# Where the weight tiles of the q/k units lie: other offsets for the second half unit in a hybrid decoder block

## The chip, the cores and the metric

The kernel runs on one core of a Trainium2 chip. The metric is the device time of one execution in microseconds (us); the time before is the median of three runs. The profile is of one further execution, and its own time stands in the table below.

## The reference, cut to what matters

One layer of a decoder block on x of 256 tokens by 2048 channels, float32: a combined input projection feeds gated linear attention (GLA, 4 heads, key width 256) and forgetting attention (FoX, 8 heads of 128); the two branches are gated, merged and projected, then a layer norm, a gated MLP with a short convolution (width 5632), a second layer norm, and a gated per-layer embedding.

```python
proj = x @ w_in                                   # (256, 2048) @ (2048, 13336)
gq, gk, gv, gr, glr, fq, fk, fv, ff, ma, mb = jnp.split(proj, offsets, axis=-1)
...
log_a = jax.nn.log_sigmoid(glr @ w_gla_lr + b_gla_lr) / GLA_TAU
o  = gla_chunked(gq / 16, gk, gv, log_a)          # GLA branch: q, k of 1024 columns each
of = fox_attention(fq, fk, fv, log_f)             # FoX branch: q, k of 1024 columns each
merged = sigmoid(ma) * (gla(o, gr) @ w_branch_gla) + sigmoid(mb) * (of @ w_branch_fox)
x = layer_norm(ALPHA * x + merged @ w_out)
x = layer_norm(ALPHA * x + (gelu(conv(x @ w_gate)) * (x @ w_up)) @ w_down)
x = x + sigmoid(x @ w_ple_gate) * (p @ w_ple_proj)
```

The change touches how the columns fq, fk, gq and gk of the projection are computed.

## The kernel before

**Precision.** Each float32 product is made of three products of shorter operands. An array v is split into hi, a copy rounded to the type float32r, and lo = v - hi; the product is hi x hi plus hi x lo plus lo x hi. The activations are kept split: tile xT holds for each of the 16 blocks of 128 channels 512 columns, the 256 tokens' hi and beside it their lo. x1T is the same for the MLP's input.

**Units.** All large weights come as units of 128 x 2048 float32 (1 MB), in the order of use, numbered u: 0 to 15 the FoX q and k columns (one q unit and one k unit per head), 16 to 31 the GLA q and k columns (two q, two k per head), 32 to 51 merge gates, then GLA values and output gates, the other merge gates, branch projections, the output projection, from 136 on gate and up columns of the MLP in turn (the first three before the main loop over them), from 224 on the down projection and the embedding's gate. `prep` loads a unit in two halves of 1024 columns. For each half SP issues a DMA into a "raw" slot, ScalarE (ACT) copies it to a hi tile (the helper of line 130), and VectorE (DVE) subtracts to make the lo tile (line 255). `unit` hands out a unit and first prepares up to three ahead. The hi and the lo tiles have pools of their own with six slots each; a slot is 1088 float32 wide (4352 bytes, 17 times 256) for a tile of 1024, and `place(u)` says how many elements into its slot the tile begins. That is all that `place` does.

**The offsets before.** `place` gives (16, 4) elements, that is 64 bytes for hi and 16 bytes for lo, to the q/k units (0 to 31) and to the gate and up units from 139 on; (0, 60), 0 and 240 bytes, to every fourteenth of these, called TURN; (0, 16) to units 136 to 138; and (0, 0) to the rest.

**The matmuls of a q/k or gate/up unit.** `w_unit` uses the weights as stationary operand (what a weight load brings into the array) and the activations as moving operand. For each of 16 blocks there is a pair: `high`, with a hi slice of 128 x 128, streams all 512 columns of the activations (line 320); `low`, with the lo slice, streams the 256 hi columns (line 325). Blocks 0 to 7 read the first half's tiles, blocks 8 to 15 the second half's. A slice is 512 bytes wide. A TURN unit does six pairs, then the remaining low matmuls, then the remaining high ones. Merge gates, branch projections and the down projection work the other way round: activations stationary, weights moving (line 1007 for the merge gates).

**What is slipped in.** In the q/k units a `tick` after the eighth pair of a unit (block 7) runs one step of a generator on the same engines: first the GLA gates (line 582), then the FoX heads (logits line 622, transposes line 649, values lines 656 and 658), then the levels of GLA's attention matrix (line 763). Some steps have matmuls, others don't. The order on TensorE is that of the program; SP's queue of transfers is in program order too. `comb` adds the two halves of a unit's result when it is complete.

Of the kernel before, what the change touches and what calls it, by code (L numbers as in the profile page):

```python
# [36 lines left out]


TURN = range(139, 224, 14)


def place(u):
    if 32 <= u < 136 or u >= 224:
        return 0, 0
    if 136 <= u < 139:
        return 0, 16
    return (0, 60) if u in TURN else (16, 4)


P_STAT = 5000  # L50
# [37 lines left out]
def tile_block(ctx: ExitStack, tc: tile.TileContext, wu, wfv, wpp, xT_in, x_in, pT_in, wlr,  # L88
# [28 lines left out]
    def t1(name):  # L117
        return sm.tile([P, 256], F32, tag="t1", bufs=6, name=name)
# [41 lines left out]
    hS = {}  # L160

    def lo_tile(u, name):
        o = place(u)[1]
        return rlo.tile([P, 1088], F32R, tag="lo", name=f"lo{name}")[:, o:o + 1024]

    def hi_tile(u, name):
        o = place(u)[0]
        return rhi.tile([P, 1088], F32R, tag="hi", name=f"hi{name}")[:, o:o + 1024]

    def differences(r0, r1, h, pinned=False):  # L170
# [28 lines left out]
    def prep_s(u):  # L199
# [25 lines left out]
        def split(src, name, e=slice(0, 1024)):  # L225
            hi = hi_tile(u, f"{u}_{name}")[:, e]
            lo = lo_tile(u, f"{u}_{name}")[:, e]
            copy(hi, src)
            nc.vector.tensor_tensor(lo, src, hi.bitcast(F32), ALU.subtract)  # L229
            return [(hi[:, o:o + 512], lo[:, o:o + 512]) for o in range(0, src.shape[1], 512)]  # L230
# [11 lines left out]
    def prep(pinned=False):  # L242
        u = n_prep[0]
        n_prep[0] += 1
        if u in s_units:
            prep_s(u)
            return
        his, los = [], []
        for h in range(2):
            raw = ring.tile([P, 1024], F32, tag="raw", bufs=5, name=f"raw{u}_{h}")  # L250
            nc.sync.dma_start(raw, wu[u, :, h * 1024:(h + 1) * 1024])
            hi = hi_tile(u, f"{u}_{h}")
            copy(hi, raw)
            lo = lo_tile(u, f"{u}_{h}")
            i = nc.vector.tensor_tensor(lo, raw, hi.bitcast(F32), ALU.subtract)  # L255
            if pinned:
                tc.keep_in_program_order(i)
            his.append(hi)
            los.append(lo)
        ready[u] = (his, los)  # L260
# [53 lines left out]
    def w_unit(ps, hi, lo, act, kts, first, last, tick=None):  # L314
# [13 lines left out]

        turn = n_used[0] - 1 in TURN
        pairs = 6 if turn else n  # L330
# [155 lines left out]
    for u in range(8):  # L486
        hi, lo = fvu[u]
        for j in range(2):
# [8 lines left out]
            for t, i, c in seq:  # L497
                o, n = fch[c]
# [181 lines left out]
    for n in range(16):  # L680
        h, j = n // 2, n % 2
# [115 lines left out]
    for n in range(16):  # L797
        nm, dst, sc = (("q", gq, 1.0 / 16.0), ("k", gk, 1.0))[n // 2 % 2]
        h, c = n // 4, n % 2
# [648 lines left out]
    for n in range(NF):  # L1448
# [18 lines left out]
        u = t1("up")  # L1467
# [4 lines left out]
        if pair in DN_S[0]:  # L1472
            if j == 0:
                yp = t2("yp").rearrange("p (k t) -> p k t", t=S)
            h = yp[:, j, :]
        else:
            h = y
# [4 lines left out]
        if pair in DN_S[0] and j == 1:  # L1482
            v = s_sums(yp)
            for i in range(2):
# [5 lines left out]
                o = k % 2 * 1024 + 512 * i  # L1490
# [295 lines left out]
```

## Time and profile before

| | |
|---|---|
| median of three runs (lowest, highest) | 1636.01 us (1635.70, 1637.37) |
| the profiled execution, its own time | 1635.61 us |
| its span on the core | 1633.8 us |
| TensorE matmuls, busy | 1627.3 us, 100% of the span |
| VectorE busy | 1343.7 us, 82% |
| ScalarE busy | 933.6 us, 57% |
| q/k units 0 to 31 on TensorE | 50.9 to 246.6 us |
| gate and up units 139 to 223 on TensorE | 846.3 to 1309.4 us |

How to read it: PE is TensorE's matmuls, PEld its weight loads, which run beside matmuls. A matmul's duration is longer than its share of time, since matmuls overlap: a 512-column matmul lasts some 390 ns, but the next one starts some 227 ns after it. What counts is the distance from one start to the next, so the rows of the timeline (start, then duration, both in us) are read by the difference of starts. In rows that group instructions by line, the numbers after the bar are busy time in us and the mean duration in ns, then the idle time before them. A name such as psfq<-xT,hi means: tile psfq is written from xT and hi; psfq, psfk are results of FoX q/k units, psq, psk of GLA q/k units, psg, psu of gate and up units, psm of merge gates.

### The profile page before, as it was taken

To read this page: it belongs to the slowest core of one execution; us is meant where nothing else is said; L and a number is where in the kernel's file an instruction comes from. 1 tells how busy PE (TensorE), PEld (TensorE's weight loads), DVE (VectorE), ACT (ScalarE), POOL (GpSimd) and SP (SyncE) were. 2 spreads that over 40 slices of the span, in tenths; PEclk is the share of its full clock that TensorE was granted. 3 is DMA by queue.
4 is the path that set the end of the run, shared out by engine and by line. 5 is a ranking of instruction groups with operands and counts; after the bars stand their busy time and mean duration, and the time that the engine had idled before them with its cause. 6 is when DMAs were issued, how large, how long until landed. Compare 5 with 4: busy or idle time off the path is not lost.

```text
span 1633.8 us, 23487 instructions
## 1 busy us (share of the span) xinstructions
PE 1627.3 (100%) x8422; PEld 1395.0 (85%) x8422; DVE 1343.7 (82%) x1920; ACT 933.6 (57%) x1321; POOL 93.0 (6%) x244
## 2 busy tenths in 40 slices
PE   9999999999999999999999999999999999999998
PEld 8988888888888888888898888888888888888887
DVE  7698899788989867879986887888777688988887
ACT  6655555456666653546575554665555555556554
POOL 0000000000000000000010111111110000000000
PEclk9999999999999999999999999999999999999999
DMA  9799899878898758889856887989776688899574
GB/s 328 286 371 340 295 388 352 294 261 305 305 349 299 250 191 322 299 321 389 300 187 198 323 309 284 350 305 357 280 239 222 201 285 326 305 351 355 168 261 152
DMA packets 114838, 477.81 MB, mean 292 GB/s; under 512 B 13032, under 2 KB 14320, under 8 KB 95136
## 3 DMA queue, kind: packets, MB, share of 16 engines
q1 hardware_dynamic: 105216, 417.57, 72.0%
q0 software_dynamic: 9504, 58.73, 9.0%
q8 instruction: 66, 1.08, 0.3%
q14 instruction: 52, 0.43, 0.1%
HBM read 417.53 MB, written 58.73 MB: 291 GB/s over the span
## 4 chain that ended last, share of the span: by engine, by line
PE 99%; DVE 0%; ACT 0%; DMA 0%; POOL 0%; issue 0%; SPq 0%; ACTq 0%
PE psm L1007 11%; PE dn L869 10%; PE psu L320 10%; PE psg L320 9%; PE psa L1007 5%; PE psu L325 5%; PE psg L325 5%; PE dn_p L869 4%; PE wo L869 3%; PE gr L869 3%; PE gv L869 3%; PE pg L381 3%; PE psb L1007 3%; PE fv L500 3%; PE gr_p L869 2%; PE gv_p L869 2%
## 5 line engine op out<-in xcount | busy, mean ns | idle before, releaser
L255 DVE TENSOR_TENSOR lo<-raw,hi 128x1024 fp32r<-128x1024 f32 x456 | 552.2, 1220 | 129.6 <-ACT hi L130 128.4
L130 ACT ACTIVATE hi<-raw 128x1024 fp32r<-128x1024 f32 x456 | 477.1, 1057 | 294.8 <-PE psg L320 59.3
L320 PE MATMUL psg<-x1T,hi 128*128 128x512 f32 x672 | 230.5, 389 | 0.0
L320 PE MATMUL psu<-x1T,hi 128*128 128x512 f32 x688 | 229.6, 390 | 0.0
L325 PE MATMUL psg<-x1T,lo 128*128 128x256 f32 x672 | 185.7, 276 | 0.0
L325 PE MATMUL psu<-x1T,lo 128*128 128x256 f32 x688 | 180.1, 277 | 0.0
L1007 PE MATMUL psm<-hi,xT 128*128 128x512 f32 x512 | 163.1, 392 | 0.0
L320 PEld LDWEIGHTS psu<-x1T,hi 128*128 128x128 f32 x688 | 128.7, 188 | 26.4
L320 PEld LDWEIGHTS psg<-x1T,hi 128*128 128x128 f32 x672 | 126.2, 188 | 26.1
L130 ACT ACTIVATE hi_b<-raw 128x512 fp32r<-128x512 f32 x112 | 93.6, 842 | 73.6 <-DMA raw<-in_wu_dram 19.9
L325 PEld LDWEIGHTS psg<-x1T,lo 128*128 128x128 f32 x672 | 126.1, 188 | 0.0
L325 PEld LDWEIGHTS psu<-x1T,lo 128*128 128x128 f32 x688 | 125.2, 188 | 0.6
L229 DVE TENSOR_TENSOR lo_b<-raw,hi_b 128x512 fp32r<-128x512 f32 x112 | 105.2, 953 | 18.9 <-ACT hi_b L130 18.4
L172 DVE TENSOR_TENSOR td<-td 128x512 f32<-128x512 f32 x172 | 117.9, 685 | 1.2
L1007 PEld LDWEIGHTS psm<-hi,xT 128*128 128x128 f32 x512 | 96.2, 188 | 19.6
L229 DVE TENSOR_TENSOR lo_t<-td,hi_t 128x1024 fp32r<-128x1024 f32 x86 | 101.7, 1219 | 7.6 <-ACT hi_t L130 6.9
L130 ACT ACTIVATE hi_t<-td 128x1024 fp32r<-128x1024 f32 x86 | 88.5, 1053 | 21.0 <-DMA td<-td 12.0
L1007 PE MATMUL psm<-lo,xT 128*128 128x512 f32 x256 | 99.9, 390 | 0.0
L869 PE MATMUL dn<-hi,hC 128*128 128x512 f32 x352 | 97.8, 389 | 0.0
L1007 PE MATMUL psa<-hi,oT 128*128 128x512 f32 x256 | 81.2, 392 | 0.0
L869 PEld LDWEIGHTS dn<-hi,hC 128*128 128x128 f32 x352 | 66.0, 188 | 13.7
L1464 DVE SCALAR_TENSOR_TENSOR yc<-gp,chn,yc 128x256 f32<-128x256 f32 x88 | 42.5, 483 | 21.3 <-ACT yc L1459 15.5
(414 smaller groups left out, 3140.3 us busy)
## 6 DMA issues: line engine op xcount, KB each, us to landing
raw<-in_wu_dram SPq DMA_DIRECT2D x525, 512.0 KB, 6.1
td<-in_wu_dram SPq DMA_DIRECT2D x43, 1024.0 KB, 8.7
td<-td POOLq DMA_DIRECT2D x43, 1024.0 KB, 7.7
td<-td SPq DMA_DIRECT2D x43, 1024.0 KB, 7.9
hS<-sd SPq DMA_DIRECT2D x11, 1024.0 KB, 8.7
raw<-in_wu_dram SPq DMA_DIRECT2D x43, 256.0 KB, 6.5
fvraw<-in_wfv_dram SPq DMA_DIRECT2D x13, 524.0 KB, 7.1
sd<-hs POOLq DMA_DIRECT2D x24, 256.0 KB, 6.6
```

Source lines behind the costliest of these rows:

```text
L130: return nc.scalar.activation(o, i, AF.Copy, bias=0.0, scale=scale)
L172: sub = lambda o, a, b: nc.vector.tensor_tensor(o, a, b, ALU.subtract)
L229: nc.vector.tensor_tensor(lo, src, hi.bitcast(F32), ALU.subtract)
L255: i = nc.vector.tensor_tensor(lo, raw, hi.bitcast(F32), ALU.subtract)
L320: nc.tensor.matmul(ps, lhsT=hi[i // 8][:, i % 8 * P:i % 8 * P + P], rhs=act[kts[i] // 4][:, kts[i] % 4, :], start=first and i == 0, stop=l ...
L325: nc.tensor.matmul(ps[:, 256:512], lhsT=lo[i // 8][:, i % 8 * P:i % 8 * P + P], rhs=act[kts[i] // 4][:, kts[i] % 4, 0:256], start=False, s ...
L381: nc.tensor.matmul(bs[j][:, 0:m], lhsT=x, rhs=v[:, o:o + m], start=first and i == 0, stop=last and i == 2)
L500: nc.tensor.matmul(fbk[t][c][:, 0:n], lhsT=x, rhs=w[:, o:o + n], start=kt == 0 and i == 0, stop=kt == 15 and i == 2)
L869: nc.tensor.matmul(ps[:, e], lhsT=x, rhs=w, start=k == 1, stop=k == total.get(id(ps), 3 * ns))
L1007: nc.tensor.matmul(ps[t], lhsT=x, rhs=v, start=first and i == 0 and j == 0, stop=last and i == 3 and j == 2)
L1464: nc.vector.scalar_tensor_tensor(y3, tap, cw[j], y3, ALU.mult, ALU.add)
```

## The change

In the q/k units the two tiles of the second half unit begin elsewhere in their slots. The hi tile goes from 64 to 192 bytes. The lo tile goes from 16 bytes to 0 in units 0, 1, 4, 5, 8, 9 and so on, and stays at 16 bytes in units 2, 3, 6, 7, 10, 11 and so on. The first halves, all other units, and the number, order and shapes of all instructions are as they were. A half is known by its tile's name, which ends in `_1` for the second half of a unit prepared by `prep`.

```diff
 TURN = range(139, 224, 14)
-
-
-def place(u):
+SECOND = ((48, 0), (48, 4))
+
+
+def place(u, h=0):
     if 32 <= u < 136 or u >= 224:
         return 0, 0
     if 136 <= u < 139:
         return 0, 16
-    return (0, 60) if u in TURN else (16, 4)
+    if u in TURN:
+        return 0, 60
+    return SECOND[u // 2 % 2] if h and u < 32 else (16, 4)
...
     def lo_tile(u, name):
-        o = place(u)[1]
+        o = place(u, name[-2:] == "_1")[1]
         return rlo.tile([P, 1088], F32R, tag="lo", name=f"lo{name}")[:, o:o + 1024]

     def hi_tile(u, name):
-        o = place(u)[0]
+        o = place(u, name[-2:] == "_1")[0]
         return rhi.tile([P, 1088], F32R, tag="hi", name=f"hi{name}")[:, o:o + 1024]
```

## The prediction

> **What bounds the kernel now.** I read the page's busy line and its chain of waits first, to see which engine sets the end.
>
> ```profile
> PE 1627.3 (100%) x8422; PEld 1395.0 (85%) x8422; DVE 1343.7 (82%) x1920; ACT 933.6 (57%) x1321; POOL 93.0 (6%) x244
> PEclk9999999999999999999999999999999999999999
> PE 99%; DVE 0%; ACT 0%; DMA 0%; POOL 0%; issue 0%; SPq 0%; ACTq 0%
> ```
>
> TensorE (PE) is busy for the whole span, at its full granted clock, and 99% of the chain that ended last is its own matmuls. So a change moves the time only if it moves the spacing at which matmuls start one after another, or if it makes TensorE wait. The second is nearly absent; the view of TensorE's waits has two rows, both from the first microseconds:
>
> ```profile
> PE warm_ps L140 <- DVE warm L137: 1.2, 1, 1.2
> PE fv L500 <- ACT fvhi L130: 0.6, 1, 0.6
> ```
>
> Next I read the stage that the change touches, the 32 q/k units, from 50.9 to 246.6 us. A unit is 16 pairs of a "hi" matmul of 512 columns (line 320) and a "lo" matmul of 256 (line 325). The groups by line inside that window, with their mean duration in ns:
>
> ```profile
> L320 PE MATMUL psfk<-xT,hi 128*128 128x512 f32 x128 | 44.5, 391 | 0.0
> L325 PE MATMUL psfq<-xT,lo 128*128 128x256 f32 x128 | 35.8, 279 | 0.0
> L325 PE MATMUL psk<-xT,lo 128*128 128x256 f32 x128 | 35.8, 279 | 0.0
> L325 PE MATMUL psq<-xT,lo 128*128 128x256 f32 x128 | 35.7, 279 | 0.0
> L325 PE MATMUL psfk<-xT,lo 128*128 128x256 f32 x128 | 35.7, 279 | 0.0
> ```
>
> and the same two instructions in the gate and up units, from the view of tile psu (minimum/median/maximum):
>
> ```profile
> L320 PE MATMUL psu<-x1T,hi x688: 387/389/398, 846.3 to 1309.1; 128*128 128x512 f32 x172
> L325 PE MATMUL psu<-x1T,lo x688: 273/276/284, 846.6 to 1309.3; 128*128 128x256 f32 x172
> ```
>
> The same shapes, placed at the same offsets (64 bytes for hi, 16 for lo), last 389 and 276 ns there, and 391 and 279 on average here. The timeline shows that this mean is a mixture of two levels. These rows are the starts of units, and one stretch in the middle of a unit where other matmuls are slipped in (start in us, then duration):
>
> ```profile
> 81.29 0.39 PE L320 MATMUL psfk<-xT,hi 128*128 128x512 f32 x1
> 86.73 0.39 PE L320 MATMUL psfq<-xT,hi 128*128 128x512 f32 x1
> ...
> 89.45 0.49 PE L649 MATMUL pt<-ident,lg 128*128 128x128 f32 x3
> 89.78 0.82 PE L622 MATMUL pl<-fqk 128*128 128x128 f32 x4
> ...
> 93.22 0.39 PE L320 MATMUL psfk<-xT,hi 128*128 128x512 f32 x1
> 98.76 0.39 PE L320 MATMUL psfq<-xT,hi 128*128 128x512 f32 x1
> ...
> 199.26 0.39 PE L320 MATMUL psq<-xT,hi 128*128 128x512 f32 x1
> 204.81 0.39 PE L320 MATMUL psq<-xT,hi 128*128 128x512 f32 x1
> ...
> 211.25 0.39 PE L320 MATMUL psk<-xT,hi 128*128 128x512 f32 x1
> 216.80 0.39 PE L320 MATMUL psk<-xT,hi 128*128 128x512 f32 x1
> ```
>
> Unit 5 takes 86.73 - 81.29 = 5.44 us, or 340 ns a pair. Unit 7 takes 98.76 - 93.22 = 5.54 us, or 346 ns a pair; units 24 and 26 take 5.55 us, 347 a pair. I call these the short and the long level, 6.8 ns apart. Between units 5 and 7 lie the seven matmuls of a FoX step, slipped into unit 6 after its eighth pair, exactly where its second half begins. The level changes only at such places, and then stays. Followed through the timeline, the long level holds in 20 of the 32 first halves and in 22 of the 32 second halves: the second halves of units 0 to 3, 6, 7, 10, 11, 14, 15, 18 to 20 and 23 to 31. The means agree: 279 lies three quarters of the way from 276 to 280 (rounded), 42 of 64 is 0.66.
>
> That fixes what is at stake. A half unit has 8 pairs, so the long level costs 22 x 8 x 6.8 ns = 1.20 us in the second halves and 20 x 8 x 6.8 = 1.09 us in the first ones. If all of it went, 2.3 us or 0.14% would be won.
>
> **The change, part by part.** It adds, removes and moves no instruction, wait or transfer. In units 0 to 31 only, the second half's hi tile starts 192 instead of 64 bytes into its slot, and its lo tile 0 bytes (two units) and then 16 bytes (the next two), in turn, instead of always 16. All slots are 4352 bytes, 17 times 256, and the sliced weights step by 512 bytes, so the position modulo 256 against the activations is the same for every pair of a half. Three things read or write these tiles.
>
> First, the writers: 32 of ScalarE's copies and 32 of VectorE's subtractions, one for each tile that moves. Their groups in the same window:
>
> ```profile
> L255 DVE TENSOR_TENSOR lo<-raw,hi 128x1024 fp32r<-128x1024 f32 x65 | 78.8, 1219 | 8.4 <-ACT hi L130 8.2
> L130 ACT ACTIVATE hi<-raw 128x1024 fp32r<-128x1024 f32 x65 | 67.6, 1055 | 31.0 <-issue 12.4 <-DMA raw<-in_wu_dram 6.2 <-PE psq L320 3.1
> ```
>
> On the page the same two groups, over 456 tiles of all placements, have means of 1220 and 1057 ns; the offsets 64 and 0 for hi, and 16 and 0 for lo, are both among them. I cost the writers at nothing. Their cover is that units are prepared up to three ahead, some 16 us of matmuls. If a writer became even 50 ns slower, 32 of them would cost VectorE 1.6 us over a stage in which it has 8.4 us of idle time ahead of this group alone.
>
> Second, the two changes of address per unit. The kernel has such jumps already: the turn units among the gate and up units, every fourteenth, have their tiles at 0 and 240 bytes. The start of one such unit, of its sixth pair, of the unit after it and of the next:
>
> ```profile
> 922.59 0.39 PE L320 MATMUL psu<-x1T,hi 128*128 128x512 f32 x1
> 924.32 0.39 PE L320 MATMUL psu<-x1T,hi 128*128 128x512 f32 x1
> ...
> 928.12 0.39 PE L320 MATMUL psg<-x1T,hi 128*128 128x512 f32 x1
> 933.57 0.39 PE L320 MATMUL psu<-x1T,hi 128*128 128x512 f32 x1
> ```
>
> Five pairs take 1.73 us, 346 ns each, with nothing added at the jump itself, and the next unit is back at 340. I cost the jumps at nothing; one long pair each, 64 x 6.8 ns, would be 0.4 us and goes into the upper end.
>
> Third, the pace after the jump. The turn unit's first six pairs are the same instructions in the same order as in the units around it, and only their addresses differ: this is the one row that shows the address choosing the level. No row has a hi tile at 192 as stationary operand, so the pace is bounded. Each pair seen with any placement lies at 340 or 346 to 347. Equal positions do no harm by themselves where a merge gate streams its weights at 0 against activations at 0:
>
> ```profile
> 248.20 0.39 PE L1007 MATMUL psm<-lo,xT 128*128 128x512 f32 x1
> ...
> 251.60 0.39 PE L1007 MATMUL psm<-lo,xT 128*128 128x512 f32 x1
> ```
>
> There are 15 matmuls from the first row to the second, 3.40 us, 227 ns each, the pace of the hi matmul at the short level. So the lower bound for a second half is the short level in all 22 long ones, -1.20 us, or -2.3 us if the first halves that follow inherit it. The upper bound within the levels seen is the long level in the 10 second halves that are short now, +10 x 8 x 6.8 = +0.54 us, or with the 12 short first halves +1.2 us. Beyond the levels seen, one further step of 6.8 ns on all 256 pairs adds 1.7 us.
>
> Which value? The level belongs to a combination of the address and of a state that the slipped-in matmuls leave behind. At 64 and 16 one state is short and the other long; in the state in which 64 and 16 is short, moving the tiles by -64 and -32 bytes made it long. I take the turn row as the nearest: a move of this size exchanges the levels. Then 22 second halves become short and 10 become long: (10 - 22) x 8 x 6.8 ns = -0.65 us, with first halves as they are.
>
> The sum: the profiled execution took 1635.61 us, of which 1633.8 is the span and 1.8 lies around it; the span becomes 1633.15 and the execution 1634.96. The median of the three runs, 1636.01, lies 0.40 above that execution, so the median becomes 1635.36, said as 1635.4. The runs spread from 1635.70 to 1637.37, more than the effect. A difference under 0.2%, 3.27 us, is about what a measurement of this kernel can't tell from no change.
>
> [...] Two levels occur for one shape here, 340 and 347 ns a pair. [...]
>
> **The rivals.**
>
> All gain: second halves are short in both states, and the halves behind them may follow. For it: 340 is a stable pace at three of the eight FoX k units and all ordinary gate and up units. Against: the only jump seen made things longer. It gives -1.2 us (1634.8), with the first halves -2.3 us (1633.7).
>
> Nothing: the level follows the slipped-in matmuls alone. For it: every change of level in this stage happens there, at fixed addresses. Against: the turn units. It gives 1636.0.
>
> Slower: the second half's lo tile at 0 stands exactly where the activations stand, and hi at 192 is no better, so second halves are long in either state. The place is units 4, 5, 8, 9, 12, 13, 16, 17, 21 and 22, short now; the price is 0.54 us, 1.2 us with the first halves behind them (1636.6 to 1637.2). It ends above 1636.0 as soon as more short halves turn long than long ones turn short. A third level one step above the long one would cost 22 x 8 x 6.8 + 10 x 8 x 13.6 = 2.3 us (1638.3), with the jumps 2.7, and two steps 4.0 us (1640.0); only from about 11 ns per pair over the long level is 0.2% passed. Against a third level: none of the 16-pair units on the timeline shows one.
>
> The far one: q/k units end up to 2 us earlier or later and leave the later gate and up units at the long level. The stretch has 85 units, 78 of them not turn units, 0.1 us each: +7.8 us, 1643.8. Against it: each of the six turn units that another gate or up unit follows has that unit at 340, so the state is set anew there, and the merge gates, matmuls of another form, lie between.
>
> **How the numbers follow.** Levels exchanged, 1635.4: 0.34. All gain, 1633.7 to 1634.8: 0.27. Nothing, 1636.0: 0.17. Slower within the two levels, 1636.6 to 1637.2: 0.13. A third level, 1638.3 to 1640: 0.06. The far one: 0.01. A gain over 0.2% by something not seen here: 0.02. The range runs from the full gain less half of the runs' spread below the median (1633.7 - 0.3 = 1633.4) to the first third level with its jumps (1636.0 + 2.7 = 1638.7), which leaves out less than 2 in 10. Within 0.2% (1632.7 to 1639.3) lie the first four cases and most of the fifth: faster 0.03, same 0.92, slower 0.05.
>
> **What would show it.** In the changed kernel's timeline, second halves of units 6, 7, 10, 11, 14, 15 and 24 to 31 should be at 340 ns a pair (hi 389, lo 276), those of units 4, 5, 8, 9, 12, 13 at 347 (hi 392, lo 280), and the window of the q/k units should shrink from 195.7 to about 195.0 us. ScalarE's and VectorE's means should stay at 1055 and 1219, the gate and up units at 5.44 us, and TensorE should wait for nothing. The prediction is wrong in its cause if halves keep the level they have, if a pace other than 340 or 347 appears, or if the time moves outside this window; it is wrong in its time if a pair costs 11 ns more than the long level.

## The result, and the profile after

Over 22 runs of each kernel the median goes from 1635.85 to 1634.01 us, 1.84 us less. The ratio is 0.9987, with a 95% interval of 0.9982 to 0.9993. That is a gain, and smaller than 0.2%. The forecast was 1635.4, and the range around it, 1633.4 to 1638.7, holds the result; but what happened on the chip was not what the forecast rested on. It was one of the rivals, "all gain".

The profiled execution took 1634.05 us, with a span of 1632.2 us (1635.61 and 1633.8 before). The page's busy line and chain of waits after the change:

```profile
PE 1626.2 (100%) x8422; PEld 1395.0 (85%) x8422; DVE 1344.1 (82%) x1920; ACT 936.0 (57%) x1321; POOL 92.0 (6%) x244
PE 99%; DVE 0%; ACT 0%; POOL 0%; issue 0%; ACTq 0%
```

TensorE is still the bound, with as many matmuls as before. The groups by line inside the window of the q/k units (three lines were added ahead of it, so line 320 is now 323 and 325 is 328):

```profile
L323 PE MATMUL psfk<-xT,hi 128*128 128x512 f32 x128 | 44.0, 389 | 0.0
L328 PE MATMUL psfq<-xT,lo 128*128 128x256 f32 x128 | 35.5, 277 | 0.0
L328 PE MATMUL psq<-xT,lo 128*128 128x256 f32 x128 | 35.4, 276 | 0.0
L328 PE MATMUL psk<-xT,lo 128*128 128x256 f32 x128 | 35.4, 276 | 0.0
```

The mean of hi in psfk is 389 where it was 391, and lo has 276 to 277 where it had 279: the mixture of two levels is gone and the short one is left. The timeline shows the same at places shown of the kernel before, the starts of units 7, 8, 24 and 25:

```profile
93.16 0.39 PE L323 MATMUL psfk<-xT,hi 128*128 128x512 f32 x1
...
98.60 0.39 PE L323 MATMUL psfq<-xT,hi 128*128 128x512 f32 x1
...
198.51 0.39 PE L323 MATMUL psq<-xT,hi 128*128 128x512 f32 x1
...
203.95 0.39 PE L323 MATMUL psq<-xT,hi 128*128 128x512 f32 x1
```

Units 7 and 24 take 5.44 us each where they took 5.54 and 5.55; both halves of each had been long. Now all 64 half units end at the short pace, judged by their last three pairs, where 42 ended long. The window from the first q/k matmul to the first merge gate, in the kernel before (the stretch, its length, then TensorE's busy time, its clock, the DMA share and GB/s):

```profile
50.94:246.59 195.65, 195.51 (x1164) 1.00 0.90 334
```

and in the changed kernel:

```profile
51.34:245.03 193.69, 193.55 (x1164) 1.00 0.91 338
```

The q/k units take 193.69 us instead of 195.65, 1.96 less. That is the whole of the change: the start, before any q/k unit, is 0.40 longer in this execution (51.34 against 50.94), and 1.96 less 0.40 is the 1.56 us between the two profiled executions. The start lies anywhere from 50.9 to 51.7 in the kernels below, of which none touches it, and the stretch between the q/k units and the gate and up units takes 599.5 to 601.0. So lengths of stretches are compared here, and single times only where a stretch doesn't say enough.

### The profile page after: what moved, and what is told of

It is laid out like the page before. It is cut to its first block, busy times and chain, and to the rows that moved or that the text cites. A ratio compares the mean times of both kernels' runs of the same rounds, so it can differ in the third digit from the quotient of the medians.

```text
span 1632.2 us, 23487 instructions
## 1 busy us (share of the span) xinstructions
PE 1626.2 (100%) x8422; PEld 1395.0 (85%) x8422; DVE 1344.1 (82%) x1920; ACT 936.0 (57%) x1321; POOL 92.0 (6%) x244
## 4 chain that ended last, share of the span: by engine, by line
PE 99%; DVE 0%; ACT 0%; POOL 0%; issue 0%; ACTq 0%
PE psm L1010 11%; PE dn L872 10%; PE psu L323 10%; PE psg L323 9%; PE psa L1010 5%; PE psu L328 5%; PE psg L328 5%; PE dn_p L872 4%; PE wo L872 3%; PE gr L872 3%; PE gv L872 3%; PE fv L503 3%; PE pg L384 3%; PE psb L1010 3%; PE gr_p L872 2%; PE gv_p L872 2%
## 5 line engine op out<-in xcount | busy, mean ns | idle before, releaser
L232 DVE TENSOR_TENSOR lo_t<-td,hi_t 128x1024 fp32r<-128x1024 f32 x86 | 101.8, 1220 | 12.1 <-ACT hi_t L133 11.3
L133 ACT ACTIVATE hi_t<-td 128x1024 fp32r<-128x1024 f32 x86 | 88.4, 1055 | 29.3 <-DMA td<-td 18.9
```

What stands on the lines that cost most here:

```text
L133: return nc.scalar.activation(o, i, AF.Copy, bias=0.0, scale=scale)
```

## The experiments

Each table of offsets is given as hi, lo in elements (4 bytes). A half unit is called long or short by its last three pairs. The theory after the result, called A in the expectations, is that a tile at 192 doesn't sustain the long pace, whatever brought it about, and that the first halves inherit the short one; its rivals are that lo's alternation does it (L), or any jump of address (J).

**Hi alone, and lo alone.** The first edit undoes lo's alternation, the second undoes the move of hi:

```diff
-SECOND = ((48, 0), (48, 4))
+SECOND = ((48, 4), (48, 4))      # hi_alone
+SECOND = ((16, 0), (16, 4))      # lo_alone
```

> Second halves of the q/k units: hi at 192 bytes, lo at 16 in all (the alternation of lo is undone). Theory A (a hi tile at 192 does not hold the long pace of 347 ns a pair, whatever the state, and the first halves at 64 and 16 inherit the short pace): the q/k units take 193.7 us as in the changed kernel, 0 of 64 half units end at the long pace. Theory L (lo has to follow the state, hi does not matter): the units whose lo is moved back, 0, 1, 4, 5, 8, 9 and so on, end long again, up to 16 second and 16 first halves, 32 x 8 x 6.8 ns = 1.7 us: 195.4 us. Theory J (any jump of address inside a unit sets the pace anew): 193.7 us.

> Second halves of the q/k units: hi back at 64 bytes, lo at 0 and 16 in turn by pair of units (the move of hi is undone). Theory A: nothing of the gain is left, 195.6 us, about 42 of 64 half units long; at most those where lo jumps gain. Theory L: the whole gain, 193.7 us, 0 long. Theory J: gain where there is a jump, in the 16 units with lo at 0, and the halves that follow until the next slipped-in matmuls: about half of the gain, 194.7 us.

The q/k window with hi alone:

```profile
50.96:244.71 193.75, 193.61 (x1164) 1.00 0.90 338
```

and with lo alone:

```profile
51.67:247.37 195.70, 195.56 (x1163) 1.00 0.90 335
```

With hi alone, 193.75 us and no half long: the whole gain, with times of 1633.74 against 1635.68 for the kernel before beside it. With lo alone, 195.70 us: nothing. So the alternation of lo gains nothing, with hi at 192 or without. Lo at 0 with hi at 64 even has a third pace, in 10 of the 16 second halves that stand so; the other 6 are short, as they were before. This is unit 9 with lo alone, its second half and the start of unit 10:

```profile
109.29 0.39 PE L323 MATMUL psfk<-xT,hi 128*128 128x512 f32 x1
...
112.09 0.39 PE L323 MATMUL psfq<-xT,hi 128*128 128x512 f32 x1
```

Eight pairs take 2.80 us, 350 ns each, longer than the long level. Theory L fell, and so did half of J, by which lo's jump would have gained something.

**Is it the jump, or the place?** The first edit puts both halves at 192, so that nothing jumps; the second puts the first half there and the second back.

```diff
-    return SECOND[u // 2 % 2] if h and u < 32 else (16, 4)
+    return (48, 4) if u < 32 else (16, 4)                # no_jump
+    return (48, 4) if not h and u < 32 else (16, 4)      # first_half
```

> Both halves of the q/k units at 192 and 16 bytes: no jump of address inside a unit or between units. Theory A: 193.7 us within 0.3, 0 half units long. Theory J: as before the change, 195.6 us, some 42 half units long, since nothing jumps.

> The first halves of the q/k units at 192 and 16 bytes, the second halves back at 64 and 16: the same jumps at the same places as with hi alone moved in the second half, the other way round. Theory A: a second half behind slipped-in matmuls that leave the long pace stays long for its 8 pairs and the next first half ends it: up to some 12 second halves long, no first half, 193.7 + 12 x 8 x 6.8 ns = 194.3 us. Theory J: 193.7 us, 0 long.

The q/k window without a jump:

```profile
51.68:245.60 193.92, 193.78 (x1163) 1.00 0.91 336
```

and with the halves exchanged:

```profile
51.45:245.96 194.51, 194.37 (x1163) 1.00 0.90 335
```

Without any jump the q/k units take 193.92 us, and two of 64 halves do not run short to their end by the same measure. (The execution as a whole took 1635.43 us all the same: its start is 0.7 longer, and TensorE waits 0.8 us for VectorE between the q/k and the gate and up units.) With the halves exchanged 194.51, and 15 second halves long, where some 12 were expected; no first half is at 347 (two, behind slipped-in work, are at 353). Unit 8 of the latter shows it in one unit: the second half after the slipped-in matmuls from its second pair, the next unit, and that unit's second half.

```profile
103.76 0.39 PE L323 MATMUL psfq<-xT,hi 128*128 128x512 f32 x1
...
106.19 0.39 PE L323 MATMUL psfk<-xT,hi 128*128 128x512 f32 x1
...
108.92 0.39 PE L323 MATMUL psfk<-xT,hi 128*128 128x512 f32 x1
```

Seven pairs at 64 and 16 take 2.43 us, 347 ns each, and go on so to the end of the unit. Then eight pairs at 192 and 16 take 2.73, 341 each. The jump from 192 to 64 in the middle set nothing right; the tile at 192 did. Theory J is out.

Theory A needs a limit, though. The two halves not at the short pace without a jump are the first halves of units 0 and 23, and with the halves exchanged they are the two at 353. In both units matmuls are slipped in at the start as well as after the eighth pair: two after the first pair of unit 0, four ahead of unit 23. These are the fifth and the eighth pair of unit 23 without a jump:

```profile
193.99 0.40 PE L323 MATMUL psk<-xT,hi 128*128 128x512 f32 x1
...
195.05 0.40 PE L323 MATMUL psk<-xT,hi 128*128 128x512 f32 x1
```

Three pairs take 1.06 us, 353 ns each, with hi at 192 and lo at 16. Unit 0 without a jump is short in its last two pairs; the other three of these four halves are at 351 to 354 from the fifth pair to the end. So 192 ends the pace of 347, but behind some slipped-in work it can have a slow pace of its own, 351 to 354 ns, for the rest of a half. Unit 21, which also begins behind slipped-in matmuls, is short again from its fourth pair on; what parts these cases is open.

**Any other place than 64, or a fixed distance?** Hi at 128 with lo at 16; and both tiles moved by 128 bytes, so that they stand to each other as before:

```diff
+SECOND = ((32, 4), (32, 4))      # hi_128
+SECOND = ((48, 36), (48, 36))    # both_moved
```

> Second halves of the q/k units: hi at 128, lo at 16 bytes. Theory N (the hi tile has only to leave the neighbourhood of 64 bytes): 193.7 to 193.9 us, 0 half units long. Rival Q (192 alone, three quarters of the way round the 256 bytes, is good): the long pace stays at least where it was, 195.6 us, or a third pace appears as with lo at 0 and hi at 64 (350 ns a pair).

> Second halves of the q/k units: hi at 192 and lo at 144 bytes, so that both are moved by 128 and stand to one another as at 64 and 16 before. Theory X (what matters is each tile's place against the activations that stream meanwhile, hi's above all): short again or a pace of its own set by lo at 144; not the before pattern. Rival D (what matters is the distance between the hi and the lo tile, 48 bytes): the pattern of before in the second halves, long where they were long, some 22 of 32, and 195.6 us.

The q/k window with hi at 128:

```profile
51.56:248.10 196.54, 196.40 (x1163) 1.00 0.90 333
```

and with both moved:

```profile
51.39:246.82 195.43, 195.29 (x1163) 1.00 0.90 334
```

Hi at 128 is worse than before, 196.54 us: all 32 second halves run at 351 to 353 ns. So a move away from 64 is not enough, and theory N fell; of rival Q, the third pace came. With both moved, 19 second halves end at 351 ns and the others short. The time, 195.43 us against 195.6, would suit rival D. But none of them is at 347, and they are others than before (units 8, 9, 12, 13, 16 and 17 are among them, which were short, and units 0 to 3 are not, which were long), so the distance between the two tiles alone does not decide (rival D fell). Hi at 192 alone is not enough: with lo at 144 it has a slow pace of its own, those 351 ns.

**What exchanges the levels.** In the kernel before, each of the eight FoX steps that have transposes, with 7 or 11 matmuls, exchanged the two levels. (Seven of them follow the eighth pair of a unit, one stands between units 20 and 21.) The next kernel has the old offsets and one transpose more, never read, in each of these steps:

```diff
+            nc.tensor.transpose(pt[:, 384:512], lg[:, 0:P], ident)
```

> All q/k tiles at 64 and 16 bytes as before the change, and one more transpose (never read) in each of the eight FoX steps that have transposes, so that the slipped-in matmuls of those steps number 8 or 12 instead of 7 or 11; 8 x 0.11 us of work more. Theory P (an odd number of slipped-in matmuls exchanges the two paces, as if hi and lo changed places in something that alternates): from unit 5 to unit 19 the pace no longer changes; if it enters short, 0 of those 30 half units are long where 13 were, and the q/k units take about 195.6 us. Rival T (the moment at which the pairs start again decides): the pace goes on changing every two units, some 13 to 17 of them long.

Between units 5 and 19, 15 half units were long in the kernel before (the expectation's 13 was miscounted), in turns of two units. With even counts they are short up to the first half of unit 8, go long at the first step of 12, and stay long through unit 22. The q/k window:

```profile
51.66:248.86 197.20, 197.06 (x1172) 1.00 0.90 333
```

The q/k units took 197.2 us, of which 0.9 is the eight transposes; it entered unit 5 short, and for that case theory P expected 195.6. So one slipped-in matmul more does matter: of the eight steps one exchanged the level where all eight had, 23 of the 30 half units are long in one block, and the turns of two units, which rival T expected to go on, are gone. But that one step was even, where theory P expected none to exchange the level, and in the kernel before three even steps did (in units 0, 4 and 23). Parity alone is not the rule.

**A stretch with nothing slipped in.** The gate and up units stand at 64 and 16 in the changed kernel too, with a turn unit every fourteenth. The first edit takes the turn units away; the second also puts the second halves' hi tiles at 192 there:

```diff
-TURN = range(139, 224, 14)
+TURN = range(0)                                          # no_turn and no_turn_192
-    return SECOND[u // 2 % 2] if h and u < 32 else (16, 4)
+    return (48, 4) if h else (16, 4)                     # no_turn_192
```

> The changed kernel with no turn units: all 85 gate and up units at 64 and 16 bytes, pairs throughout. A turn unit takes 0.093 us more than an ordinary one, so 7 x 0.093 = 0.65 us go. Theory A says that at 64 and 16 either pace holds once it is there: the stretch of gate and up units (463.06 us) takes 462.4 us if it begins short and 463.06 - 0.65 + 85 x 16 x 0.0068 = 471.7 us if it begins long, and does not change in between, since nothing is slipped in. Rival: it starts short and falls to the long pace somewhere on its own: between the two.

> No turn units, and hi at 192 and lo at 16 bytes in the second halves of the q/k units and of the gate and up units. Theory A: short everywhere, with no turn unit needed: q/k units 193.7 us, gate and up units 462.4 us, the whole 0.65 us below the changed kernel, some 1633.4 us. Rival: in the long stretch without slipped-in matmuls the short pace is lost even with hi at 192, and the stretch takes more than 463 us.

The view of tile psu without turn units (minimum/median/maximum):

```profile
L323 PE MATMUL psu<-x1T,hi x688: 392/392/392, 845.1 to 1316.3; 128*128 128x512 f32 x172
L328 PE MATMUL psu<-x1T,lo x688: 280/280/281, 845.4 to 1316.5; 128*128 128x256 f32 x172
```

and with hi at 192 as well:

```profile
L323 PE MATMUL psu<-x1T,hi x688: 389/389/394, 844.5 to 1306.6; 128*128 128x512 f32 x172
L328 PE MATMUL psu<-x1T,lo x688: 276/276/280, 844.7 to 1306.8; 128*128 128x256 f32 x172
```

The window of the 85 gate and up units in the changed kernel:

```profile
844.69:1307.75 463.06, 463.06 (x2723) 1.00 0.78 277
```

without turn units:

```profile
845.14:1316.61 471.47, 471.47 (x2723) 1.00 0.76 272
```

and without them, with hi at 192:

```profile
844.49:1306.94 462.45, 462.45 (x2722) 1.00 0.78 277
```

Without turn units the stretch begins long and stays so for all 85 units: not one hi matmul is below 392 ns, and it takes 471.47 us where 471.7 was expected. With the hi tiles of the second halves at 192 it is short from the second unit on, 462.45 us where 462.4 was expected. Between these two the program is the same but for the offsets. So the turn units, which cost 0.6 us, are what brought this stretch to the short pace, and the tile at 192 does the same at no cost.

**The better version, timed, and a try beyond it.**

> The version of no turn units with hi at 192 and lo at 16 bytes in the second halves of the q/k units and of the gate and up units, timed. Theory A: 1635.9 - 1.9 (q/k units) - 0.6 (turn units) = 1633.4 us, a ratio of 0.9985 to the kernel before, below the changed kernel's 0.9987; with the short pace in every ordinary pair. Rival (the pace in the long stretch is lost in some executions): single executions up to 8 us longer.

> The kernel above, and units 136 to 138 (the three prepared before the main loop of the gated MLP, whose matmuls have 256 columns) at 192 and 16 bytes in place of 0 and 64. Theory X: the hi tile at 0 is what makes their matmuls start some 119 ns apart instead of the 113 of a lo matmul in a short pair; 144 matmuls x 6 ns = 0.9 us go from the stretch of about 19 us that begins with the first of them. Rival: their activations are read in two pieces of 128 columns, which costs the same wherever the weights lie: no change.

The version without turn units and with hi at 192 has a median of 1633.29 us over 11 runs beside 1636.26 for the kernel before; the ratio is 0.9983, interval 0.9973 to 0.9992. The interval overlaps the changed kernel's, so the times alone don't part the two; the stretch of 462.45 against 463.06 us does. No execution was above 1634.78, so none lost the short pace over a large part of the long stretch, which over the whole of it costs 9.0 us (471.47 against 462.45).

The last kernel has units 136 to 138 at 192 and 16 as well:

```diff
-        return 0, 16
+        return 48, 4
```

Its single execution took 1632.76 us, but the stretch it was meant for, from the first of those matmuls to the first unit of the main loop, only went from 19.09 to 18.92: 0.17 us of the 0.9. Most of those 256-column matmuls still start 116 to 121 ns apart, so the offset of hi was not what holds most of them; whether it is the two pieces in which they read their activations was not tried by itself.

## Why the prediction was right and wrong, step by step

**Right: the bound and the stake.** TensorE had no wait to lose, the two levels and their 6.8 ns carried the stage, and the whole of the change lies in the q/k window. 42 long half units were put at 2.3 us; 1.96 came. Most of the rest is in what follows the slipped-in matmuls. The second half of unit 8 in the kernel before, from its second pair to the next unit, was short:

```profile
103.52 0.39 PE L320 MATMUL psfq<-xT,hi 128*128 128x512 f32 x1
...
105.90 0.39 PE L320 MATMUL psfk<-xT,hi 128*128 128x512 f32 x1
```

The same half in the changed kernel, its first three pairs and the next unit:

```profile
102.77 0.58 PE L323 MATMUL psfq<-xT,hi 128*128 128x512 f32 x1
...
103.31 0.40 PE L323 MATMUL psfq<-xT,hi 128*128 128x512 f32 x1
...
103.66 0.40 PE L323 MATMUL psfq<-xT,hi 128*128 128x512 f32 x1
...
105.72 0.39 PE L323 MATMUL psfk<-xT,hi 128*128 128x512 f32 x1
```

Before, seven pairs took 2.38 us, 340 ns each. In the changed kernel the first pair, behind the slipped-in work, is 0.54 us as before. The next two take some 352 ns each, longer than the long level, and the remaining five are at 340 to 341: (105.72 - 103.31 - 2 x 0.352) / 5. So where a second half had been short, the tile at 192 adds a disturbance of two or three pairs; it leaves it after them. Over all half units the second to fourth pairs together take 0.32 us more than at 340 ns.

**Right: costs put at nothing.** The writers' means in the window are 1057 and 1220 ns (1055 and 1219 before), TensorE waits for 0.2 us in the whole span after the first microseconds, and the gate and up units take 463.06 us, as before.

**Wrong: the value chosen for the pace after the jump.** The prediction's third step took the turn row as the nearest and let a move of this size exchange the levels in both states, -22 and +10 second halves, -0.65 us. The row it took as nearest was not near: the turn units move hi by 64 bytes and lo by 32, the change moves hi by 128 and lo by 16 or by nothing. The 10 did not turn long, and the 20 long first halves, which the forecast left as they were, became short too, though nothing moved there. The turn row, 346 ns a pair at 0 and 240, showed that an address can choose the level; it did not show that the choice is an exchange. What the runs showed in its place: at 64 and 16 both paces, 340 and 347 ns, hold once they are there; with the second halves at 192 and 16 (hi_alone) none of the 64 halves ends at 347, and a first half behind them takes over the 340. That was the lower bound of the sum, -2.3 us, and the rival "all gain" with the halves behind them. How a half with hi at 192 would run, no row could tell. That the first halves behind would follow, the rows did tell: the prediction itself noted that the level changes at slipped-in matmuls only and then stays, also across units, so the sum should not have left the first halves as they were.

By its own signs the prediction was wrong in its cause: the second halves of units 4, 5, 8, 9, 12 and 13 kept the short level, and the window shrank to 193.7 us and not to about 195.0. That the time fell inside the range, and on the side that was forecast, was luck as far as the reasoning goes: an exchange gains only because more second halves were long (22) than short (10), and the range held the result because a rival was in it.

**What the place of the weights did.** Without turn units the same matmuls last 392 and 280 ns with the second halves' hi tiles at 64, and 389 and 276 with them at 192 (medians over 85 units on end). The step from 340 to 347 ns is 2% of a pair, and with hi at 128 it is 3.5% (352 against 340). So on this kernel the position of the weights matters, by these 2 to 3.5%. Whether the read of the weights is what holds the matmuls up, no run here shows.

**The rivals that did not come.** The gate and up units kept their short pace (the far rival), and of the third level, 350 to 353 ns, the changed kernel shows only the two or three pairs behind slipped-in matmuls. It does exist as a lasting pace, at other offsets.

## What to carry to other kernels

When one engine is busy throughout, compare the start-to-start distance of the same instruction in different stages: here a mean of 391 and 279 ns, between 389 and 276 and 392 and 280, was a mixture, and the timeline said where it switched. A pace that held once it was there, 347 ns a pair, was ended by one part of the loop that does not sustain it, and the parts behind it inherited the result; so look for a setting at which only the good pace lasts, not for the right setting in each state. When a change has two parts, run each alone: here the move of lo gained nothing, and the move of hi gained everything.

## What the runs showed of the hardware

Pairs of a 512- and a 256-column matmul with float32r weights start 340, 347 or 350 to 353 ns apart, and in these runs the pace went with where the hi and lo tiles begin in their slots. The slots are 17 x 256 bytes wide and the slices 512, and the pace is the same from slot to slot over 85 units (without turn units all 1360 hi matmuls of the gate and up units last 392 ns), so the place is given in bytes modulo 256; no run moved the activations. 64 and 16 hold 340 or 347, whichever they come to (units 5 and 7 of the kernel before); 192 and 16, and 192 and 0, end at 340 (hi_alone and the changed kernel), but for the first halves named above (no_jump and first_half, up to 353 with 192 and 16); 64 and 0 end at 350 in 10 of 16 cases and at 340 in the others (lo_alone); 128 and 16 at 351 to 353 (hi_128); 192 and 144 at 340 or 351 (both_moved). Why one place sustains a pace and another doesn't is open, and so is the full rule by which slipped-in matmuls exchange the paces.
